# A decoder layer with 32 experts: order kept on chip, transfers of other rows set apart, last norms interleaved

## The chip, the core and the metric

The kernel runs on one core of a Trainium2 chip. The metric is the device time of one execution in microseconds, as the median of several. Engines: TensorE (PE), VectorE (DVE), ScalarE (ACT), GpSimd (POOL) and the queue of SyncE (SP). POOL issues the indirect DMAs (gathers and scatters by a list of row numbers), SP the plain ones.

## The reference

One layer: a projection, a pooling and a recurrent mixer, an output product with a layer norm (h), then a mixture of experts and a second layer norm. The change lies in the last two.

```python
def hierarchical_moe(h, ...):          # h: 4096 rows of 1024
    g_prob = softmax(h @ router_group + b_g)
    g_top_p, g_idx = lax.top_k(g_prob, 1)              # 1 of 4 groups
...
    e_top_logit, e_idx = lax.top_k(e_sel, 2)           # 2 of its 8 experts
    weights = g_top_p * softmax(e_top_logit)
...
    hid = silu(xb @ exp_gate[e]) * (xb @ exp_up[e])
    return (hid @ exp_down[e]) * wgt
...
h = layer_norm(ALPHA * x + mixed, ln1_g, ln1_b)
return layer_norm(ALPHA * h + hierarchical_moe(h), ln2_g, ln2_b)
```

## The kernel before

**Router.** `phase_out` goes over 32 blocks of 128 rows: two output products, the norm of h, then (one block later) transposes and the router's products. Each block writes h to `d_h` and ALPHA times h to `d_acc`. After a batch of blocks (`BATCHES`) `route` works out each row's group, two experts and weights on DVE, counts with two PE products, and POOL scatters small rows: (token, weight) into a table per expert (`d_tab`, two scatters a block) and the token into a list per group (`d_gtab`, one a block). The tiles `ids` and `row` that feed them have two buffers. Before the last batch `plan.order` ranks groups and experts by their counts so far; the ranks go out to `d_order` in memory and come back into `orow`, from which SP and POOL read which expert comes next.

**Experts.** `phase_moe` goes over the 32 ranks in a written order (`manual_schedule`): each engine runs the instructions in the order in which the code calls them. `GIVEN` and `GGIVEN` say how many blocks of 64 rows an expert of a rank, and of 128 rows a group, gets. For expert r: `fetch` gathers up to two blocks of finished rows of the group before from `d_acc` into `f_h`; `hidden` makes p_gu on PE, and in its gaps scales and stores (`out_dram`) the blocks fetched one expert earlier; `down` makes p_y, ACT evicts it to y, `scatter` adds y onto `d_acc`; beside it the rows of the next expert, gathered as `xg` (three buffers), are transposed on PE (m_pt) into xh (ACT) and xl (DVE), and DVE takes the statistics (`f_st`) of the fetched blocks. PE needs the last xl before the next p_gu.

The framework orders two accesses of `d_acc` by a wait unless told that they don't meet:

```python
def free(ins, others, reason):
    for other in others:
        if other is not last_pool[0]:
            tc.declare_no_dep(ins.ins, other.ins, reason=reason)
```

So each transfer still waits for the landing of the one issued just ahead of it.

**Last norms.** The last group has no expert after it: four blocks of it are fetched, and the six of `GGIVEN[-1]` are normalised one by one, with 1/sqrt as Ln and Exp on ACT (`log_root`, a table load before each), b2 added on POOL, a store, and one more fetch. Two loops that follow, for rows beyond the given counts, run zero times here; their branches make all engines meet.

## Time and profile before

| | |
|---|---|
| median of 3 runs | 3928.93 us (3922.88 to 3951.8) |
| profiled execution | 3922.84 us, span 3921.2 us, mean granted clock 0.883 |
| 0 to 2500: projection, mixer | PE busy 2178.37 us |
| 2500 to 2900: output product, router | PE busy 391.71 us, DMA share 0.64 |
| 2900 to 3000: end of router, first expert | PE busy 36.25 us, clock 0.61 |
| 3000 to 3850: experts | PE busy 739.96 us, clock 0.94, DMA share 0.79 |
| 3850 to 3921: last norms | PE busy 3.87 us, DVE 18.27, ACT 28.56, POOL 29.65 |

Stretches are in us from the span's start. The clock is the share of full speed that the throttle granted to PE, the DMA share the mean busy share of 16 DMA engines. In rows, the time in brackets is how long the engine was idle before the instruction, and behind the arrow what ended that; where it waited for several things the one named is the last by the profile.

### The profile page before, as it was taken

How to read it: one execution, taken by the hardware profiler on the slowest of the kernel's cores; microseconds unless marked ns; L12 is line 12 of the kernel's file. 1: busy time of each engine (PE TensorE's matmuls, PEld its weight loads, DVE VectorE, ACT ScalarE, POOL GpSimd, SP SyncE). 2: the span in 40 equal slices, each digit the busy share in tenths (PEclk: the TensorE clock that was granted, in tenths of full speed). 3: DMA queues.
4: the chain of work that ended last, by engine and by line, in shares of the span. 5: the costliest groups of instructions: out<-in, count | busy, mean ns of one | idle time of the engine just before them, and what ended most of it. 6: DMA issues, size and time to landing. Idle time of an engine off the chain costs nothing. (4 is left out here: it accounts for less than half of the span.)

```text
span 3921.2 us, 70586 instructions
## 1 busy us (share of the span) xinstructions
PE 3350.2 (85%) x27401; PEld 2801.9 (71%) x27401; DVE 1999.1 (51%) x4077; ACT 1620.8 (41%) x2718; POOL 1696.2 (43%) x2985
## 2 busy tenths in 40 slices
PE   7999999999857888888788886899976999697872
PEld 6887877777646776777677775677755898586762
DVE  2212231222256777667676673566553557546674
ACT  2212111111135455554545443565643555455444
POOL 3000030000157778777777783143432234534344
PEclk9999999999967788777878777999987999898886
DMA  7424252332223333343333323567636888777873
GB/s 253 177 116 182 99 186 102 119 127 94 68 57 72 84 73 83 68 87 70 80 76 75 86 57 94 185 142 156 145 76 180 214 232 260 225 218 231 233 235 101
DMA packets 509753, 531.22 MB, mean 135 GB/s; under 512 B 297853, under 2 KB 411687, under 8 KB 505320
## 3 DMA queue, kind: packets, MB, share of 16 engines
q1 hardware_dynamic: 445752, 367.94, 33.3%
q0 software_dynamic: 33920, 106.02, 10.8%
q10 hardware_dynamic: 29744, 52.73, 3.7%
q8 instruction: 216, 3.54, 0.4%
q14 instruction: 121, 0.99, 0.1%
HBM read 324.90 MB, written 206.92 MB: 136 GB/s over the span
## 5 line engine op out<-in xcount | busy, mean ns | idle before, releaser
L134 PE MATMUL acc<-xhi,wh 128*128 128x512 f32 x1408 | 565.8, 402 | 4.2 <-DVE zo L176 3.9
L135 PE MATMUL acc<-xlo,wh 128*128 128x512 f32 x1408 | 559.4, 397 | 0.0
L136 PE MATMUL acc<-xhi,wl 128*128 128x512 f32 x1408 | 559.4, 397 | 0.0
L491 POOL TENSOR_TENSOR db<-db,tmp 96x126 f32<-96x126 f32 (+22 forms) x992 | 456.4, 460 | 77.7
L176 DVE SCALAR_TENSOR_TENSOR zo<-acc,omu,zm 128x512 f32<-128x512 f32 x160 | 119.9, 750 | 661.1 <-ACT zm L173 617.7
L489 POOL TENSOR_TENSOR tmp<-db,gi 96x126 f32<-96x126 f32 (+22 forms) x992 | 423.1, 427 | 77.7
L173 ACT ACTIVATE zm<-acc,muc 128x512 f32<-128x512 f32 x160 | 110.2, 690 | 719.2 <-PE acc L136 717.9
L174 POOL COPY carry<-zm 128x1 f32<-128x1 f32 x160 | 30.8, 193 | 664.3 <-ACT zm L173 664.2
L134 PEld LDWEIGHTS acc<-xhi,wh 128*128 128x128 f32 x1408 | 265.4, 189 | 70.9 <-DVE zo L176 4.2
L135 PEld LDWEIGHTS acc<-xlo,wh 128*128 128x128 f32 x1408 | 265.7, 189 | 66.6 <-issue 3.8
L136 PEld LDWEIGHTS acc<-xhi,wl 128*128 128x128 f32 x1408 | 265.4, 188 | 63.4
L1262 POOL DMA_INDIRECT d_acc<-y,ix x81 | 136.9, 1690 | 282.6 <-DMA d_acc<-y,ix 73.2
L1061 PE MATMUL o_ps<-owh,mh 128*128 128x512 f32 x512 | 210.0, 411 | 18.1 <-ACT owh L889 17.6
L1314 PE MATMUL p_gu<-xl,wh_g 128*128 128x256 f32 (+4 forms) x512 | 159.2, 311 | 72.5 <-DVE xl L1293 72.5
L1061 PE MATMUL o_ps<-owh,ml 128*128 128x512 f32 x512 | 205.4, 401 | 5.0 <-POOL ml L876 5.0
L1061 PE MATMUL o_ps<-owl,mh 128*128 128x512 f32 x512 | 204.9, 401 | 0.4 <-DVE owl L890 0.3
L445 DVE TENSOR_TENSOR g<-tr,mask 128x384 f32<-128x384 f32 x256 | 130.2, 549 | 143.2 <-PE tr L443 143.2
L443 PE MATMUL tr<-ar,kb 64*128 64x128 f32 x1536 | 178.5, 364 | 25.5 <-DVE kb L430 17.4
L443 PEld LDWEIGHTS tr<-ar,kb 64*128 64x128 f32 x1536 | 147.3, 252 | 46.5 <-DVE g L445 17.3
L370 ACT ACTIVATE thw<-tr,chans 128x256 f32<-128x256 f32 x96 | 45.6, 475 | 297.6 <-PE tr L369 263.8
L1349 PE MATMUL p_y<-wh_d,hh 128*128 128x512 f32 (+1 forms) x324 | 145.5, 449 | 15.0 <-ACT hh L1324 15.0
L1314 PE MATMUL p_gu<-xh,wh_u 128*128 128x256 f32 (+4 forms) x512 | 157.9, 308 | 0.0
(354 smaller groups left out, 8704.1 us busy)
## 6 DMA issues: line engine op xcount, KB each, us to landing
d_rkv<-zo SPq DMA_DIRECT2D x144, 256.0 KB
ws<-in_exp_gate_dram SPq DMA_DIRECT2D x64, 512.0 KB
ws<-in_exp_up_dram SPq DMA_DIRECT2D x64, 512.0 KB
ws<-in_exp_down_dram SPq DMA_DIRECT2D x64, 512.0 KB
xq<-in_x_dram SPq DMA_DIRECT2D x32, 512.0 KB
d_xsp<-xhi ACTq DMA_DIRECT2D x8, 2048.0 KB
d_xsp<-xlo ACTq DMA_DIRECT2D x8, 2048.0 KB
xlo<-d_xsp SPq DMA_DIRECT2D x8, 2048.0 KB
```

The costliest lines, as they stand in the source:

```text
L134: nc.tensor.matmul(ps, lhsT=whi[i][:, k, :], rhs=xhi[:, k, :], start=k == 0, stop=False)
L135: nc.tensor.matmul(ps, lhsT=whi[i][:, k, :], rhs=xlo[:, k, :], start=False, stop=False)
L136: nc.tensor.matmul(ps, lhsT=wlo[i][:, k, :], rhs=xhi[:, k, :], start=False, stop=k == KD - 1)
L176: nc.vector.scalar_tensor_tensor(zo, ps, omu[:, ix:ix + 1], zm[:, :SEG], op0=OP.mult, op1=OP.add)
L443: nc.tensor.matmul(ps[h][:, p, :], lhsT=KB[hs, i, :], rhs=AR[hs, i, :], start=True, stop=True)
L445: nc.vector.tensor_tensor(G[:, h, c::NC, :], ps[h], masks[c % 2].unsqueeze(1).to_broadcast([128, 3, 128]), op=OP.mult)
L489: e.tensor_tensor(tm, Dh[:, :a, x:x + 1].to_broadcast([96, a, b]), G[:, x, x + 1:].unsqueeze(1).to_broadcast([96, a, b]), op=OP.mult)
L491: e.tensor_tensor(Dh[:, :a, x + 1:], Dh[:, :a, x + 1:], tm, op=OP.add)
L1061: nc.tensor.matmul(ps, lhsT=a[:, k, :], rhs=w[k][:, ns], start=k == 0 and i == 0, stop=k == KD - 1 and i == 2)
L1262: st = nc.gpsimd.indirect_dma_start(out=acc, out_offset=bass.IndirectOffsetOnAxis(ap=ix[:n, 0:1], axis=0), in_=y[:n], in_offset=None, boun ...
L1314: nc.tensor.matmul(p[:, :N], lhsT=a[:, k, fs], rhs=c[:, k, :N], start=k == 0 and i == 0, stop=k == KD - 1 and i == 2)
L1349: nc.tensor.matmul(ps[j][:a1 - a0], lhsT=x[:, a0:a1], rhs=w[:, f, n * 512:n * 512 + 512], start=f == 0 and i == 0, stop=f == NF - 1 and i ...
```

## The change

- `order` turns the two columns of ranks into two rows with PE products against the identity; DVE casts them into `orow` in SBUF. The trip through `d_order` goes. `BATCHES` ends 3, 3, 2 in place of 4, 3, 1, so that the order is made after 30 blocks in place of 31.
- `ids` and `row` get four buffers; the token column of `row` is one copy from a table (`token`) in place of an iota for each block and slot.
- The group-list scatters of the last two batches are put in `plan.later` and issued after the first three `xg` gathers, each behind a memset of one element.
- `free` drops the dependence on the transfer just ahead as well, and `apart` puts a memset of one element (`scr`) on POOL between two such transfers.
- The two copies of the last block's h (`keep`) stand after its transposes.
- The last group's six blocks are fetched at once, four into `f_h` and two into `y` buffers, and normalised in two threes with `root` (Newton steps on DVE, as in the other groups). b2 is added by DVE in every second block, and stores are interleaved with the second three.

```diff
-BATCHES = [4] * 7 + [3, 1]
+BATCHES = [4] * 6 + [3, 3, 2]
...
-    def order(self):
+    def order(self, ident, ps):
...
-        eoi = pool.tile([128, 2], I32, name="pl_eoi")
-        nc.vector.tensor_copy(eoi, eo)
-        nc.sync.dma_start(self.orderd, eoi)
+        for i in range(2):
+            nc.tensor.matmul(ps[:, i], lhsT=eo[:, i:i + 1], rhs=ident, start=True, stop=True)
+        nc.vector.tensor_copy(self.orow, ps)
...
-            ids = sm.tile([128, 3, QB, 1], I32, name="ids")
-            row = sm.tile([128, 2, QB, 2], I32, name="row")
+            ids = plan.pool.tile([128, 3, max(BATCHES), 1], I32, name="ids", bufs=4)
+            row = plan.pool.tile([128, 2, max(BATCHES), 2], I32, name="row", bufs=4)
+            nc.gpsimd.tensor_copy(row[:, :, :QB, 0], token[:, q0:q0 + QB].unsqueeze(1).to_broadcast([128, 2, QB]))
...
-                for q in range(QB):
-                    nc.gpsimd.iota(row[:, s, q, 0:1], pattern=[[0, 1]], base=(q0 + q) * 128, channel_multiplier=1)
...
+            for q in range(QB):
+                if q0 + QB < NQ - BATCHES[-1]:
+                    place(q)
+                else:
+                    plan.later.append(lambda q=q: place(q))
             if q0 + QB == NQ - BATCHES[-1]:
-                plan.order()
+                plan.order(ident, prt.tile([1, 2, 128], F32, name="prt"))
...
                 turn(q - LAG)
+                if q == NQ:
+                    keep(NQ - 1, h)
...
+        scr = cst.tile([1, 1], F32, name="scr")
+
+        def apart(*others):
+
+            if any(last_pool[0] is x for o in others for x in o):
+                nc.gpsimd.memset(scr, 0.0)
+
         def free(ins, others, reason):
             for other in others:
-                if other is not last_pool[0]:
-                    tc.declare_no_dep(ins.ins, other.ins, reason=reason)
+                tc.declare_no_dep(ins.ins, other.ins, reason=reason)
 
         def scatter(ix, y, n, g=None, same=()):
 
+            if g is not None:
+                apart(reads, same)
...
-            def fetch(self, n):
-                for _ in range(n):
-                    h = fp.tile([128, D], F32, name="f_h")
+            def fetch(self, n, tile=lambda i: fp.tile([128, D], F32, name="f_h")):
+                for i in range(n):
+                    h = tile(i)
+                    apart(*sums[self.g + 1:])
...
+            def put(self, h, b, add=True):
+                if add:
+                    nc.gpsimd.tensor_tensor(h, h, b2, op=OP.add)
+                else:
+                    apart(writes)
...
         for _ in range(3):
             ahead()
+        for place in plan.later:
+            nc.gpsimd.memset(scr, 0.0)
+            place()
+        last_pool[0] = None
...
-        norms.fetch(min(4, GGIVEN[-1]))
-        every = norms.new
-        while every or norms.b < GGIVEN[-1]:
-            norms.new = every[:1]
-            every = every[1:]
-            for x in norms.stats(log_root):
-                x()
...
+        tile = lambda i: fp.tile([128, D], F32, name="f_h") if i < 4 else hp.tile([128, D], F32, name="y", bufs=4)
+        while left:
+            some = min(left, 6)
+            left -= some
+            norms.fetch(some, tile)
...
+                nc.vector.tensor_tensor(h, h, g2, op=OP.mult)
+                if i % 2:
+                    nc.vector.tensor_tensor(h, h, b2, op=OP.add)
+                norms.put(h, b, i % 2 == 0)
...
+            for first in range(0, some, 3):
+                own = Norms(NG - 1, norms.ig)
+                own.new = every[first:first + 3]
+                pieces = own.stats(root)
+                n = len(own.got)
+                for i, x in enumerate(pieces):
+                    x()
+                    if i < n and ready:
+                        finish(ready.pop(0), done)
+                        done += 1
+                own.scale()
+                ready += own.got
```

**POOL among the experts.** Before, around one expert's two scatters, with the semaphores that each waits for (DMASW: an indirect DMA has landed, Activation: an eviction of y, DVE or Pool: that engine, PE: the transposes that free `xg`):

```order
L1262 DMA d_acc<-y,ix 4224x1024 [waits Activation_49]
L1262 DMA d_acc<-y,ix 4224x1024 [waits DMASW1_49,Activation_49]
L1389 DMA f_h<-d_acc,ig 128x1024 [waits DMASW2_49]
L1389 DMA f_h<-d_acc,ig 128x1024 [waits DMASW4_49]
L1432 TENSOR_TENSOR f_h<-f_h,b_28272 128x1024 [waits DVE_49]
L1433 DMA out_dram<-f_h,ig 4096x1024 [waits Pool_49]
L1248 DMA xg<-d_h,ix 128x1024 [waits DMASW6_49,PE_49]
L1248 DMA xg<-d_h,ix 128x1024 [waits DMAHW1_49,DMASW7_49,PE_49]
```

and after, at the same place in the expert's run (`L1282` is the scatter, `L1412` the gather, `L1455` the add, `L1458` the store):

```order
L1282 DMA d_acc<-y,ix 4224x1024 [waits DMASW3_49,DMASW1_49,Activation_49]
L1272 MEMSET scr 1x1
L1282 DMA d_acc<-y,ix 4224x1024 [waits DMASW2_49,Activation_49]
L1272 MEMSET scr 1x1 [waits Pool_49]
L1412 DMA f_h<-d_acc,ig 128x1024
L1412 DMA f_h<-d_acc,ig 128x1024 [waits DMASW5_49,DMASW4_49]
L1455 TENSOR_TENSOR f_h<-f_h,b_28211 128x1024 [waits DVE_49]
L1458 DMA out_dram<-f_h,ig 4096x1024 [waits Pool_49]
L1260 DMA xg<-d_h,ix 128x1024 [waits DMASW6_49,PE_49]
```

The order of transfers is the same, with a memset after each scatter. Before, the second scatter waits for the landing of the first and the first gather for that of the second; after, the second scatter waits for an older transfer and the first gather for none.

**POOL at the end of the router.** Before, from the iotas of the last but one batch on (`L1030` and `L1044` are the small scatters, `L1027` the iotas, `L1237` loads the first expert's list):

```order
L1027 IOTA row 128x1 x2
L1030 DMA d_tab<-row,ids 131072x2 x6
L1044 DMA d_gtab<-row,ids 16384x1 x3
L1030 DMA d_tab<-row,ids 131072x2 x2
L1044 DMA d_gtab<-row,ids 16384x1
L24 MEMSET m_id 128x128
L25 AFFINE_SELECT m_id<-m_id 128x128
L1196 TENSOR_LOAD orow
L1196 ISA x2
L1237 ISA
L1237 DMA ix<-d_tab 128x4x2
L1248 DMA xg<-d_h,ix 128x1024 x3
```

and after:

```order
L1032 DMA d_tab<-row,ids 131072x2 x6
L1047 DMA d_gtab<-row,ids 16384x1 x3
L1032 DMA d_tab<-row,ids 131072x2 x10
L24 MEMSET m_id 128x128
L25 AFFINE_SELECT m_id<-m_id 128x128
L1208 TENSOR_LOAD orow
L1208 ISA x2
L1249 ISA
L1249 DMA ix<-d_tab 128x4x2
L1260 DMA xg<-d_h,ix 128x1024 x3
L1500 MEMSET scr 1x1
L1047 DMA d_gtab<-row,ids 16384x1
```

The iotas that reuse the row buffer are gone from between the batches, and five group-list scatters (one of them shown) now stand between the third and the fourth `xg`, each behind a memset.

**DVE in the last norms.** Before, one block after the other:

```order
L1413 BN_STATS f_st<-f_h 128x6 x2
L1414 BN_AGGR f_mv<-f_st 128x2
L1417 SCALAR_TENSOR_TENSOR f_mr<-f_mv,f_ra 128x1
L1428 TENSOR_TENSOR f_h<-f_h,g_28271 128x1024
L1413 BN_STATS f_st<-f_h 128x6 x2
```

and after, the first three blocks (14 more small operations of the root follow, then the next block's statistics):

```order
L1436 BN_STATS f_st<-f_h 128x6 x2
L1437 BN_AGGR f_mv<-f_st 128x2
L1436 BN_STATS f_st<-f_h 128x6 x2
L1437 BN_AGGR f_mv<-f_st 128x2
L1436 BN_STATS f_st<-f_h 128x6 x2
L1437 BN_AGGR f_mv<-f_st 128x2
L1478 TENSOR_SCALAR f_va<-f_mv 128x3
L1479 TENSOR_SCALAR f_yi<-f_va 128x3
```

The statistics of three blocks now stand together ahead of one root, and no operation of ACT stands between a block's aggregation and its root.

## Rows read from the trace of the kernel before

**Rows 1.** waits in the expert phase, 2990 to 3850: engine line waited for, us, times, longest

```profile
DVE f_st L1413 <- DMA f_h<-d_acc,ig: 107.7, 25, 15.6
...
PE p_gu L1314 <- DVE xl L1293: 72.5, 13, 15.3
```

**Rows 2.** POOL's groups by line in 2990 to 3850: busy, mean ns, idle before

```profile
L1262 POOL DMA_INDIRECT d_acc<-y,ix x79 | 133.9, 1695 | 276.2 <-DMA d_acc<-y,ix 73.2 <-ACT y L1331 55.1 <-issue 45.4
...
L1389 POOL DMA_INDIRECT f_h<-d_acc,ig x28 | 29.3, 1045 | 87.8 <-DMA d_acc<-y,ix 84.7 <-issue 3.0
```

**Rows 3.** timeline of POOL, 3520 to 3550: start, us, instruction [idle before]

```profile
3524.81 1.59 POOL L1262 DMA_INDIRECT d_acc<-y,ix  x1 [0.30 <-issue]
3533.08 2.41 POOL L1262 DMA_INDIRECT d_acc<-y,ix  x1 [6.68 <-ACT wh_g L1226]
3543.40 1.43 POOL L1262 DMA_INDIRECT d_acc<-y,ix  x1 [7.90 <-ACT y L1331]
3548.30 1.00 POOL L1389 DMA_INDIRECT f_h<-d_acc,ig  x1 [3.47 <-DMA d_acc<-y,ix]
```

**Rows 4.** timeline of ACT, 3520 to 3530

```profile
3525.97 0.68 ACT L1331 ACTIVATE y<-p_y,ix 64x512 f32<-64x512 f32 x1 [0.65 <-PE p_y L1349]
```

**Rows 5.** timeline of DVE, 3550 to 3592

```profile
3552.56 1.29 DVE L1413 BATCH_NORM_STATS2 f_st<-f_h 128x6 f32<-128x512 f32 x2 [8.92 <-DMA f_h<-d_acc,ig]
...
3587.49 0.16 DVE L1449 TENSOR_SCALAR f_va<-f_mv 128x2 f32<-128x2 f32 x1
...
3590.50 0.16 DVE L1417 SCALAR_TENSOR_TENSOR f_mr<-f_mv,f_ra 128x2 f32<-128x2 f32 x1
```

**Rows 6.** timeline of PE, 3552 to 3590

```profile
3555.30 0.58 PE L1314 MATMUL p_gu<-xl,wh_g 128*128 128x256 f32 x1 [7.12 <-DVE xl L1293]
...
3587.63 0.58 PE L1314 MATMUL p_gu<-xl,wh_g 128*128 128x256 f32 x1 [12.15 <-DVE xl L1293]
```

**Rows 7.** busy time by stretch, with granted clock, DMA share and rate

```profile
3560.00:3575.00 15.00, 15.00 (x110) 13.78 (x109) 9.16 (x12) 9.29 (x16) 4.17 (x2) 1.00 0.97 314
...
3587.00:3594.00 7.00, 6.37 (x34) 6.37 (x35) 6.48 (x21) 3.26 (x4) 1.92 (x2) 0.58 0.98 243
```

**Rows 8.** DMA in 2990 to 3850, by queue

```profile
DMA packets 67955, 192.83 MB, mean 224 GB/s; under 512 B 21046, under 2 KB 21046, under 8 KB 67889
...
q0 software_dynamic: 27776, 95.81, 45.3%
q1 hardware_dynamic: 39825, 95.13, 32.8%
```

**Rows 9.** timeline of POOL, 2905 to 2985

```profile
2910.55 1.00 POOL L1030 DMA_INDIRECT d_tab<-row,ids  x1 [22.63 <-DVE rks L1040]
...
2937.67 0.20 POOL L1027 IOTA row<- 128x1 int32 x2 [11.69 <-DMA d_gtab<-row,ids]
...
2964.15 0.83 POOL L1237 DMA_DIRECT2D ix<-d_tab  x1 [8.57 <-DMA d_tab<-row,ids]
...
2977.85 0.91 POOL L1248 DMA_INDIRECT xg<-d_h,ix  x1 [7.30 <-PE m_pt L1276]
```

**Rows 10.** timeline of PE, 2930 to 2990

```profile
2975.64 4.01 PE L1276 MATMUL m_pt<-m_id,xg 128*128 128x128 f32 x20 [36.29 <-DMA ws<-in_exp_up_dram]
...
2983.96 0.74 PE L1314 MATMUL p_gu<-xh,wh_g 128*128 128x448 f32 x1
```

**Rows 11.** timeline of POOL, 3848 to 3922

```profile
3858.81 1.43 POOL L1262 DMA_INDIRECT d_acc<-y,ix  x1 [5.37 <-issue]
...
3894.88 2.33 POOL L1432 TENSOR_TENSOR f_h<-f_h,b 128x1024 f32<-128x1024 f32 x1 [3.52 <-SPq L1570]
...
3909.24 0.98 POOL L1433 DMA_INDIRECT out_dram<-f_h,ig  x1 [0.28 <-POOL f_h L1432]
```

**Rows 12.** timeline of DVE, 3848 to 3922

```profile
3867.03 1.29 DVE L1413 BATCH_NORM_STATS2 f_st<-f_h 128x6 f32<-128x512 f32 x2 [17.65 <-DMA f_h<-d_acc,ig]
...
3871.96 1.23 DVE L1428 TENSOR_TENSOR f_h<-f_h,g 128x1024 f32<-128x1024 f32 x1 [1.36 <-ACT f_h L1424]
```

More of the change, by code (lines that the diff above doesn't have):

```diff
@@ L722, with __init__ @@
 class Plan:
-    def __init__(self, tc, pool, orderd, restd):
+    def __init__(self, tc, pool, restd):
         nc = self.nc = tc.nc
-        self.pool, self.orderd, self.restd = pool, orderd, restd
+        self.pool, self.restd = pool, restd
+        self.orow = pool.tile([1, 2, 128], I32, name="orow")
+        self.later = []
         self.ones = pool.tile([128, 128], F32, name="pl_ones")
@@ L1041, in route, with place @@
             nc.vector.scalar_tensor_tensor(r, gi, float(CAP), r, op0=OP.mult, op1=OP.add)
-            nc.vector.tensor_copy(ids[:, 2, :, 0], r)
-            for q in range(QB):
+            nc.vector.tensor_copy(ids[:, 2, :QB, 0], r)
+            def place(q):
                 st = nc.gpsimd.indirect_dma_start(
@@ L1066, in norm, with keep @@
             h = state[q][3]
+            ln_rows(nc, sm, h, leps, g1, b1)
+        def keep(q, h):
             t0 = q * 128
-            ln_rows(nc, sm, h, leps, g1, b1)
             hk = hp.tile([128, KD, 128], F32, name="hk")
@@ L1119, in phase_out @@
             if 0 <= q - LAG < NQ:
+                h = state[q - LAG][3]
                 turn(q - LAG)
+                if q == NQ:
+                    keep(NQ - 1, h)
             if q < NQ:
@@ L1123, in phase_out @@
                 norm(q)
+                if q < NQ - 1:
+                    keep(q, state[q][3])
             b = q - LAG - 1
@@ L1404, in stats @@
                     return []
-                st = sm.tile([128, 2, 2, 6], F32, name="f_st")
-                mv = sm.tile([128, 2, 2], F32, name="f_mv")
-                ra = sm.tile([128, 2], F32, name="f_ra")
-                mr = sm.tile([128, 2], F32, name="f_mr")
+                st = sm.tile([128, 4, 2, 6], F32, name="f_st")
+                mv = sm.tile([128, 4, 2], F32, name="f_mv")
+                ra = sm.tile([128, 4], F32, name="f_ra")
+                mr = sm.tile([128, 4], F32, name="f_mr")
                 self.ra, self.mr = ra, mr
@@ L1428, in apply @@
                     nc.vector.tensor_tensor(h, h, g2, op=OP.mult)
+            def put(self, h, b, add=True):
[3 more added lines that the diff above has]
+                    apart(writes)
+                st = nc.gpsimd.indirect_dma_start(
+                    out=o, out_offset=bass.IndirectOffsetOnAxis(ap=self.ig[:, b:b + 1], axis=0),
+                    in_=h, in_offset=None, bounds_check=S - 1, oob_is_err=False)
+                free(st, writes, "other rows of the result")
+                last_pool[0] = st
+                writes.append(st)
             def store(self):
                 for h, b in self.got:
-                    nc.gpsimd.tensor_tensor(h, h, b2, op=OP.add)
-                    st = nc.gpsimd.indirect_dma_start(
-                        out=o, out_offset=bass.IndirectOffsetOnAxis(ap=self.ig[:, b:b + 1], axis=0),
-                        in_=h, in_offset=None, bounds_check=S - 1, oob_is_err=False)
-                    free(st, writes, "other rows of the result")
-                    last_pool[0] = st
-                    writes.append(st)
+                    self.put(h, b)
                 self.got = []
         def root(mv, ra, n):
-            va = sm.tile([128, 2], F32, name="f_va")[:, :n]
-            yi = sm.tile([128, 2], I32, name="f_yi")[:, :n]
-            tm = sm.tile([128, 2], F32, name="f_tm")[:, :n]
+            va = sm.tile([128, 4], F32, name="f_va")[:, :n]
+            yi = sm.tile([128, 4], I32, name="f_yi")[:, :n]
+            tm = sm.tile([128, 4], F32, name="f_tm")[:, :n]
             rs = ra[:, :n]
@@ L1510, in phase_moe, with finish @@
         norms = Norms(NG - 1)
-        norms.fetch(min(4, GGIVEN[-1]))
-        every = norms.new
-        while every or norms.b < GGIVEN[-1]:
-            norms.new = every[:1]
-            every = every[1:]
-            for x in norms.stats(log_root):
-                x()
-            norms.scale()
-            norms.apply()
-            norms.store()
-            if norms.b < GGIVEN[-1]:
-                norms.fetch(1)
-                every += norms.new
+        left = GGIVEN[-1]
+        tile = lambda i: fp.tile([128, D], F32, name="f_h") if i < 4 else hp.tile([128, D], F32, name="y", bufs=4)
[3 more added lines that the diff above has]
+            norms.fetch(some, tile)
+            every, ready = norms.new, []
+            norms.new = []
+            def finish(x, i):
+                h, b = x
+                nc.vector.tensor_tensor(h, h, g2, op=OP.mult)
+                if i % 2:
+                    nc.vector.tensor_tensor(h, h, b2, op=OP.add)
+                norms.put(h, b, i % 2 == 0)
+            done = 0
+            for first in range(0, some, 3):
[10 more added lines that the diff above has]
+                ready += own.got
+            for x in ready:
+                finish(x, done)
+                done += 1
         manual.close()
@@ L1573, in phase_moe @@
             again.new = [(h, None)]
-            for x in again.stats(log_root):
+            for x in again.stats(root):
                 x()
@@ L1594, in body @@
         gtab = dp.tile([NG * CAP, 1], I32, name="d_gtab")
-        orderd = dp.tile([128, 2], I32, name="d_order")
         restd = dp.tile([128, 4], I32, name="d_rest")
```

29 lines of the change are left out of this document (11 added, 18 removed).

## The prediction

> **What bounds the kernel now.** I read the table of waits over the expert phase first, because a share of busy time over the whole program mixes stages with different limits. TensorE (PE) waits 72.5 us there, 13 times, for one thing: the low halves of the next expert's rows (xl), which VectorE (DVE) writes before the first product p_gu [rows 1]. DVE is late because it runs in order and, ahead of the last xl, stands at the statistics of a fetched block (f_st), for which it waits 107.7 us in 25 pieces [rows 1].
>
> Why the fetched block is late is read from GpSimd (POOL), grouped by line: it sat idle for 276.2 us ahead of its 79 scatter-adds (d_acc, L1262) and for 87.8 us ahead of its 28 gathers (f_h, L1389) [rows 2]. The names of the releasers are to be read with care. In one stretch the three scatter-adds of an expert are issued at 3524.81, 3533.08 and 3543.40, the gather at 3548.30 [rows 3]. The last eviction of that expert's y began at 3525.97 and took 0.68 [rows 4], so ScalarE, weights and evictions named there had long been done; what is left for each scatter is the landing of the one ahead of it. The statistics start at 3552.56, after 8.92 of waiting [rows 5], and PE at 3555.30, after 7.12 [rows 6]. POOL runs one expert late, and PE pays.
>
> Two more stretches stand by themselves. Between router and experts PE is idle for 36.29 us up to the first transposes at 2975.64, and its first product is at 2983.96 [rows 10]. At the end the first statistics start at 3867.03 [rows 12] and the last store is issued at 3909.24 [rows 11]: 43 us in which nothing but six blocks is normalised, one after the other.
>
> **Part 1, the expert phase.** The change puts a memset of one element between a scatter-add and the transfer behind it, and drops the dependences on the transfer just ahead. By the order of waits, the second and third scatter of an expert and the first gather then wait for nothing newer than the expert before. In the stretch above the three scatters would go out at 3524.81, about 3526.8 and 3528.8, and the gather at about 3530.5, 18 us earlier. Even if it landed as late as 12 us after issue (an estimate from 3552.56 minus 3548.30 = 4.3 seen there, times almost three) it would be there at 3542.5, ten before DVE asks. So the 72.5 us should go nearly whole: two thirds of the DVE stall of 107.7 is what PE sees, and no other engine stands in the same place.
>
> The stall is paid a second time in the clock. After PE's wait of 12.15 that ends at 3587.63 [rows 6] the granted clock averages 0.58 over 7 us, against 1.00 in 3560 to 3575 [rows 7]: between the levels of 1.2 and 2.4 GHz, nearer the lower, so 7 x 0.42 = 2.9 us lost. Four or five of the 13 waits are long enough for that, and shorter ones lose some; I put 13 us on it. Together 72.5 + 13 = 85.
>
> The memsets are 56 on POOL. No row has a memset of one element; POOL's small operations at the boundary take 0.20 [rows 9], and POOL has 364 us of idle time in this phase, so 56 x 0.2 = 11 us is hidden. If POOL's slack were gone it would cost those 11.
>
> Against the 85 stands DMA. The transfers of the 860 us moved 192.83 MB, with 45.3% of the 16 engines' time in POOL's queue, 32.8% in SP's and 0.9% in others: 79%, or 679 us of work that does not shrink [rows 8]. In 775 us that is a share of 0.88, in 795 it is 0.85. PE ran without a gap through 3560 to 3575 at a share of 0.97 [rows 7], so 0.88 is possible but for arrivals that bunch: weights and gathers will be later than now. I take 20 off: 65. The bounds are 25 (only as much as a share of 0.81 allows) and 95 (85 and some of the waits for ScalarE, which a filled clock also shortens).
>
> One rule of the Trainium skill gives another sum. The rows say that 314 GB/s went with a share of 0.97 [rows 7], so that some 324 would be all there is for this mixture of packets. The Trainium skill's page "DMA: Bandwidth & Descriptors", section "Specifications", puts the limits at about 358 GB/s for one core's HBM traffic and 435 for the fabric. By the page 192.83 MB need no more than 539 us, DMA would never be near its limit at 249 GB/s, nothing comes off the 85, and the sum of all parts would be 3922.84 - 110 = 3813. The measured share decides against it: by the rows it is 3922.84 - 90.
>
> **Part 2, from the router to the experts.** Of the twelve small scatters of one batch the first is issued at 2910.55, each issue taking about 1 us, and POOL is released only at 2937.67, when the last of them has landed, because the next batch reuses their row buffer [rows 9]: 27.1 / 12 = 2.26 us of service each, more than their issue. DVE is held by the same buffer. Then 12 more scatters go out and the list of the first expert is loaded at 2964.15: 26.5 us, 2.2 each [rows 9]. The change gives four buffers (the wait of 11.69 goes) and takes 5 of the group-list scatters (d_gtab), four of which stand among those 12, out of the way: 4 x 2.26 = 9.0. The sum is 20.7. DVE must still do the ranking, now for two last blocks with the order ahead of them, and the expert order now costs two PE products and a DVE copy on chip in place of a round trip that was hidden; I give 3 back, so the first transposes move 17.7 earlier, to about 2958. Now the cover is gone: the five deferred scatters stand behind the third gather, ahead of the fourth. They need 5 x 2.26 = 11.3 us of the queue, where POOL before waited 7.30 for PE [rows 9]; with the part of their time that lies beyond the first gathers I charge 5.7. The first product then moves 12 earlier. The ends: 5 (the ranking comes no earlier and only the group lists leave) and 18 (the queue lets the fourth gather by).
>
> The later copies of the last block (keep behind turn), POOL's copy in place of iotas and the smaller last batches lie beside PE's products or POOL's waits; I take nothing for them, and 2 us either way within these ends if they do not.
>
> **Part 3, the last norms.** Before, from the first statistics to the end of the last store: 3909.24 + 0.98 - 3867.03 = 43.2 us [rows 11, 12]. After, DVE carries it: six blocks of statistics at 1.29 [rows 12] and 0.2 for their aggregation (an estimate from the small operations of [rows 5, 9]) = 8.9; two roots of 15 small operations, from 3587.49 to 3590.50 and 0.16 more, 3.2 each [rows 5], = 6.4; six multiplications of 1.23 [rows 12] = 7.4; three adds of the same shape = 3.7. That is 26.4. The stop at the loop's branch, 3.52 on POOL [rows 11], stays; 1.2 is waiting for ScalarE's scaling (taken from the like-sized multiplication) and 1.0 the last store: 32.1, a gain of 11. ScalarE's table loads go, but they lay in that same chain and are not counted again. The scatter ahead no longer waits 5.37 for its neighbour [rows 11]; its own eviction allows some 3 of that. With 1 back for two more gathers ahead: 13, between 6 (POOL's adds and stores still set the pace) and 16.
>
> **The sum.** 3922.84 - 65 - 12 - 13 = 3832.8 for an execution such as the profiled one. The median of the three runs is 3928.93, 6.1 above it, so the forecast is 3839.
>
> **Rivals.** (a) DMA binds: the freed engines ask for the same 679 us of transfers in less time and meet late weights. Speaks for it: 0.79 already as a mean, two queues that both matter [rows 8]. Against: the stretch at 0.97 without a gap [rows 7]. If 0.82 is all that can be held on average, the phase takes 679 / 0.82 = 828, a gain of 32, and the whole is 3922.84 - 57 + 6 = 3872. (b) The waits move rather than go: the first scatter of each expert still waits for the scatters of the expert before, and gathers still queue behind them, so POOL stays late and DVE's stall remains to nine tenths. For it: those dependences are in the new order; against: a full expert, 20 us or more, lies between. Gain 7 + 25: 3897. (c) DMA takes nothing back: a share of 0.88 is below 0.97 [rows 7], no transfer comes late, and the whole 85 is kept: 3922.84 - 110 + 6 = 3819. The limits of the Trainium skill's page, above, come to the same. (d) Slower: scatters that overlap slow each other. POOL's queue has 390 us of engine time now, the rest 290 [rows 8]. If its packets came to take k times as long, DMA alone would last the present 860 us from k = 1.46 on; at 1.7 it lasts 953, and with 25 gained elsewhere the kernel ends at 3922.84 + 68 + 6 = 3997. For it: the scatter-adds ran singly so far, so no row excludes it. Against: the wait behind them was 8 to 10 us each [rows 3] at an issue of 2, as of transfers that share the engines with weights and not of ones that fill them.
>
> **How the numbers follow.** Forecast 0.55, (a) 0.19, (b) 0.10, (c) 0.12, (d) 0.04. The range of 3795 to 3893: the low end is all three upper bounds, 95 + 18 + 16 = 129 off, less some 5 for the runs' spread; the high end all lower bounds, 25 + 5 + 6 = 36 off. It leaves out (d) and most of (b). One per cent of 3928.93, 39 us, is about what a measurement of this kernel can tell from no change, so faster begins below 3890: the forecast, (c) and nearly all of (a), 0.84; the same: (b) and the rest of (a), 0.12; slower: (d), 0.04.
>
> **What would show it.** In the profile after: DVE's wait at f_st below 20 us and PE's at p_gu for xl below 15; POOL's idle ahead of d_acc down by over half and then named after evictions; the DMA share of the phase at 0.84 to 0.88; the first product near 2972; the last store some 30 us behind the first statistics. New rows of PE waiting for weights or xg of over 20 us would mean (a), f_h still landing after DVE asks (b), a higher time for the same packets in POOL's queue (d). The prediction is wrong above all if PE's 72.5 us reappear under another name.

## The result, and the profile after

| | before | after |
|---|---|---|
| median | 3938.53 us (4 runs, 3922.88 to 3951.8) | 3837.02 us (4 runs, 3826.27 to 3845.02) |
| profiled execution | 3922.84 us, span 3921.2, clock 0.883 | 3845.02 us, span 3843.4, clock 0.888 |

The ratio is 0.9742, 95% interval 0.9689 to 0.9795: faster. The fourth run of before, 3948.14 us, was made beside the runs of after.

The two spans in stages, cut at instructions of TensorE (PE). The last two columns are a later pair of profiles from one and the same chip (runs c0 and c1, below).

| stage, us | before | after | before, c0 | after, c1 | forecast |
|---|---|---|---|---|---|
| output product, first to last o_ps | 463.4 | 480.5 | 461.9 | 460.7 | same |
| last o_ps to first p_gu | 81.3 | 72.6 | 77.7 | 67.0 | -12 |
| first p_gu to last p_y (experts) | 869.6 | 791.9 | 873.6 | 789.3 | -65 |
| last p_y to the end | 67.6 | 58.5 | 67.8 | 58.8 | -13 |

**The experts.** The table of waits of the kernel after, 2985 to 3800 (engine, line, what it waits for; us, times, longest), answers to [rows 1]:

```profile
PE p_y L1369 <- ACT hh L1344: 18.5, 15, 4.9
PE p_y L1369 <- DVE hl L1345: 16.6, 8, 2.4
...
DVE f_st L1436 <- DMA f_h<-d_acc,ig: 15.1, 3, 13.7
...
PE m_pt L1296 <- DMA xg<-d_h,ix: 9.3, 2, 7.2
...
PEld p_gu L1334 <- DVE xl L1313: 0.2, 1, 0.2
```

The 72.5 us at p_gu for xl are gone. The 15.1 at f_st lie in the last norms (the window reaches into them); among the experts VectorE (DVE) never waits for a fetched block. What PE still waits for is mainly hh and hl, the high and low halves of the hidden rows, which ACT and DVE write ahead of p_y; 7.2 of the 9.3 for a gather of xg lie ahead of the first product. GpSimd's (POOL's) groups by line, 2985 to 3800, against [rows 2]: the scatter-adds' idle time fell from 276.2 to 91.7 us and is named after evictions, the gathers' from 87.8 to 11.1. The idle time now stands ahead of xg, where POOL waits for PE's transposes: POOL is early.

```profile
L1282 POOL DMA_INDIRECT d_acc<-y,ix x81 | 126.7, 1564 | 91.7 <-ACT y L1351 79.7 <-ACT xh L1312 8.7 <-issue 3.3
L1260 POOL DMA_INDIRECT xg<-d_h,ix x76 | 82.6, 1087 | 292.9 <-PE m_pt L1296 287.1 <-issue 3.0 <-PE p_y L1369 2.7
...
L1412 POOL DMA_INDIRECT f_h<-d_acc,ig x32 | 47.1, 1473 | 11.1 <-issue 8.8 <-DMA d_acc<-y,ix 2.3
L1272 POOL MEMSET scr<- 1x1 f32 x53 | 31.2, 588 | 0.0
```

One expert on POOL's timeline, 3515 to 3550, against [rows 3]: the scatters stand 3.65 us apart instead of 8.27 and 10.32, and the gather 1.9 behind the last.

```profile
3530.59 1.62 POOL L1282 DMA_INDIRECT d_acc<-y,ix  x1 [1.05 <-ACT y L1351]
3531.63 0.61 POOL L1272 MEMSET scr<- 1x1 f32 x1
3534.24 1.59 POOL L1282 DMA_INDIRECT d_acc<-y,ix  x1 [2.00 <-ACT y L1351]
3535.26 0.61 POOL L1272 MEMSET scr<- 1x1 f32 x1
3536.13 2.04 POOL L1412 DMA_INDIRECT f_h<-d_acc,ig  x1 [0.26 <-issue]
```

DMA in 2990 to 3785, against [rows 8]: POOL's queue and SP's together 84.0% of the engines' time, the share that was forecast (0.84 to 0.88).

```profile
DMA packets 68630, 194.90 MB, mean 245 GB/s; under 512 B 21217, under 2 KB 21217, under 8 KB 68563
...
q0 software_dynamic: 28353, 97.48, 48.1%
q1 hardware_dynamic: 39922, 95.53, 35.9%
```

**The boundary.** POOL after, 2905 to 2990, and PE, 2930 to 3000, against [rows 9, 10]:

```profile
2941.13 0.96 POOL L1032 DMA_INDIRECT d_tab<-row,ids  x1 [16.20 <-DVE rks L1042]
...
2959.79 0.96 POOL L1032 DMA_INDIRECT d_tab<-row,ids  x1 [11.01 <-DVE rks L1042]
...
2968.35 0.84 POOL L1249 DMA_DIRECT2D ix<-d_tab  x1 [2.15 <-issue]
...
2974.80 1.00 POOL L1047 DMA_INDIRECT d_gtab<-row,ids  x1 [0.23 <-issue]
...
2981.41 0.93 POOL L1260 DMA_INDIRECT xg<-d_h,ix  x1 [0.51 <-issue]
```

```profile
2979.19 5.45 PE L1296 MATMUL m_pt<-m_id,xg 128*128 128x128 f32 x24 [21.61 <-POOL scr L1500]
2991.86 1.08 PE L1296 MATMUL m_pt<-m_id,xg 64*128 64x64 f32 x8 [7.22 <-DMA xg<-d_h,ix]
2992.99 0.74 PE L1334 MATMUL p_gu<-xh,wh_g 128*128 128x448 f32 x1
```

POOL no longer waits for its own scatters but for DVE's ranking (rks), and it stands idle for 2.15 us ahead of the list's load instead of 8.57. From first transposes to first product, though, 13.8 us pass instead of 8.3: the gather behind the five group lists comes last.

**The last norms.** POOL and DVE after, 3780 to 3840, against [rows 11, 12]:

```profile
3815.33 2.33 POOL L1455 TENSOR_TENSOR f_h<-f_h,b 128x1024 f32<-128x1024 f32 x1 [1.33 <-DVE f_va L1478]
...
3826.30 2.47 POOL L1455 TENSOR_TENSOR y<-y,b 128x1024 f32<-128x1024 f32 x1
3829.05 1.67 POOL L1458 DMA_INDIRECT out_dram<-y,ig  x1 [0.28 <-POOL y L1455]
...
3831.02 0.99 POOL L1458 DMA_INDIRECT out_dram<-y,ig  x1 [0.21 <-POOLq L1618]
```

```profile
3794.51 1.28 DVE L1436 BATCH_NORM_STATS2 f_st<-f_h 128x6 f32<-128x512 f32 x2 [13.74 <-DMA f_h<-d_acc,ig]
...
3800.72 0.17 DVE L1479 TENSOR_SCALAR f_yi<-f_va 128x3 int32<-128x3 int32 x1
...
3809.30 2.15 DVE L1551 TENSOR_TENSOR f_h<-f_h,g 128x1024 f32<-128x1024 f32 x1
...
3815.35 2.33 DVE L1479 TENSOR_SCALAR f_yi<-f_va 128x3 int32<-128x3 int32 x1
...
3826.61 3.24 DVE L1553 TENSOR_TENSOR y<-y,b 128x1024 f32<-128x1024 f32 x1
```

From the first statistics to the end of the last store it is 3831.02 + 0.99 - 3794.51 = 37.5 us, before 43.2, forecast 32.1. The two f_yi rows show one reason: the same operation on three numbers a partition takes 0.17 alone and 2.33 when it starts beside an addition of POOL, as long as that addition.

### The profile page after: what moved, and what is told of

The parts are those of the page before. It is cut to its first block, busy times and chain, and to the rows that moved or that the text cites. A ratio compares the mean times of both kernels' runs of the same rounds, so it can differ in the third digit from the quotient of the medians.

```text
span 3843.4 us, 70576 instructions
## 1 busy us (share of the span) xinstructions
PE 3346.6 (87%) x27405; PEld 2800.3 (73%) x27405; DVE 2041.7 (53%) x4105; ACT 1600.2 (42%) x2694; POOL 1728.8 (45%) x2988
## 3 DMA queue, kind: packets, MB, share of 16 engines
q0 software_dynamic: 33920, 106.02, 10.7%
## 5 line engine op out<-in xcount | busy, mean ns | idle before, releaser
L489 POOL TENSOR_TENSOR tmp<-db,gi 96x126 f32<-96x126 f32 (+22 forms) x992 | 430.0, 433 | 77.7
L1260 POOL DMA_INDIRECT xg<-d_h,ix x81 | 87.4, 1079 | 296.7 <-PE m_pt L1296 288.0
L443 PE MATMUL tr<-ar,kb 64*128 64x128 f32 x1536 | 180.3, 367 | 24.2 <-DVE kb L430 16.6
L1282 POOL DMA_INDIRECT d_acc<-y,ix x81 | 126.7, 1564 | 91.7 <-ACT y L1351 79.7
L879 POOL TENSOR_TENSOR ml<-m,mh 128x1024 fp32r<-128x1024 f32 x32 | 76.6, 2395 | 184.4 <-ACT mh L878 184.3
```

The source lines that it names most:

```text
L443: nc.tensor.matmul(ps[h][:, p, :], lhsT=KB[hs, i, :], rhs=AR[hs, i, :], start=True, stop=True)
L489: e.tensor_tensor(tm, Dh[:, :a, x:x + 1].to_broadcast([96, a, b]), G[:, x, x + 1:].unsqueeze(1).to_broadcast([96, a, b]), op=OP.mult)
L1282: st = nc.gpsimd.indirect_dma_start(out=acc, out_offset=bass.IndirectOffsetOnAxis(ap=ix[:n, 0:1], axis=0), in_=y[:n], in_offset=None, boun ...
```

## The experiments

Times of one group share a chip and the runs of the kernel before on it. "Experts", "boundary" and "tail" are the stages of the table.

**a1 to a4: the parts alone** (kernel before there: 3926.43). a1 is the kernel before with part 1 only:

```diff
+        scr = cst.tile([1, 1], F32, name="scr")
...
+        def apart(*others):
...
+            if any(last_pool[0] is x for o in others for x in o):
+                nc.gpsimd.memset(scr, 0.0)
...
         def free(ins, others, reason):
             for other in others:
-                if other is not last_pool[0]:
-                    tc.declare_no_dep(ins.ins, other.ins, reason=reason)
+                tc.declare_no_dep(ins.ins, other.ins, reason=reason)
...
         def scatter(ix, y, n, g=None, same=()):
...
+            if g is not None:
+                apart(reads, same)
...
                     h = fp.tile([128, D], F32, name="f_h")
+                    apart(*sums[self.g + 1:])
```

> The kernel before with the memsets and the dropped dependences alone. If the waits of POOL for landings are what holds DVE and then PE, the expert phase (first p_gu to last p_y, 870 us before, 802 after) falls to about 802 here too, DVE's wait at f_st to under 5 us, and the kernel gains 65 to 70 us (ratio about 0.983). Rival: the gain of the phase comes from the other parts or from the state of the executions; then the phase stays above 850 and the ratio above 0.99.

a2 is the kernel after without part 1, but for the stores: those of finished blocks (`out_dram`) don't wait for one another.

```diff
-        def free(ins, others, reason):
+        def free(ins, others, reason, last=False):
             for other in others:
-                tc.declare_no_dep(ins.ins, other.ins, reason=reason)
+                if last or other is not last_pool[0]:
+                    tc.declare_no_dep(ins.ins, other.ins, reason=reason)
...
-            if g is not None:
-                apart(reads, same)
...
-                    apart(*sums[self.g + 1:])
...
-                free(st, writes, "other rows of the result")
+                free(st, writes, "other rows of the result", True)
```

> The changed kernel with the dependence on the transfer just ahead kept and no memsets among the experts. If the three parts are separate, the expert phase is back at 865 to 875 us, DVE waits about 108 us at f_st and PE about 72 us for xl, and the kernel is 22 to 30 us faster than before (ratio 0.992 to 0.995). Rival: the parts overlap, and the ratio falls below 0.985 or rises to 1.

a3 is a2 with the last norms as before (`log_root`, one block after the other), a4 is a2 with the router and the boundary as before (`BATCHES`, `d_order`, iotas, no `later`).

> The kernel before with the router part alone (order on chip, batches 3, 3, 2, four row buffers, deferred group lists, copies of the last block behind its transposes). From the end of the last output product to the first p_gu: 81.1 us before, 64.2 after. If the profile's difference is the part's worth, 64 to 66 here, a gain of 12 to 18 us (ratio about 0.996). Rival: the later end of the output products in the profile after (2920 in place of 2903) belongs to this part, so that it gains nothing: ratio 0.999 to 1.003 and products that end near 2920 again.

> The kernel before with the last norms alone (six blocks fetched at once, roots on DVE, stores interleaved). From the last p_y to the end of the span: 67.2 us before, 57.5 after. Expected 57 to 59 here, a gain of 8 to 13 us (ratio 0.997). Rival: without the dropped waits the second scatter is late as before and the gain is 5 or less.

| | median us | ratio, 95% | experts | boundary | tail |
|---|---|---|---|---|---|
| a1 part 1 | 3836.24 | 0.9768, 0.9751 to 0.9784 | 786.1 | 78.0 | 64.7 |
| a2 parts 2 and 3 | 3891.11 | 0.9912, 0.9895 to 0.9928 | 860.7 | 67.6 | 61.3 |
| a3 part 2 | 3899.53 | 0.993, 0.9913 to 0.9947 | 860.7 | 67.5 | 66.9 |
| a4 part 3 | 3909.45 | 0.9955, 0.9939 to 0.9972 | 864.0 | 78.6 | 60.1 |

In the expectations of a1 and a3 the figures "after" of 802 and 64.2 us are misread: cut as in the table above, the kernel after has 791.9 and 72.6. All four kernels gained more than was expected of them: 90, 35, 27 and 17 us, where 65 to 70, 22 to 30, 12 to 18 and 8 to 13 stood.

Part 1 alone takes the experts to where the whole change has them, so they are its doing: in a1 DVE doesn't wait at f_st among the experts and PE not for xl, while in a2 to a4 PE waits 64 to 71 us for xl. No run drops the waits without the memsets, so what these do for the order isn't shown. Part 2 shortens the boundary by 10.7 us (the mean of a1 and a4 less that of a2 and a3), part 3 the tail by 5.6 (a3 to a2). Part 1 has some 2 of the tail as well (a3 to a1). The products of the ratios, 0.9768 x 0.9912 = 0.968, are less than the change's own, 0.974: the experts of a2 to a4, with part 1 out, are 6 to 13 us shorter than the 870 to 874 of before, and the product counts that twice. That is a part of the some 22 us between the two; the rest stays open. The stores' wait that they drop is the only piece of part 1 that all three share; that it makes those us was not tried apart.

**b0 to b3** (kernel before there: 3945.84). b0 is the kernel after once more.

> The changed kernel once more, beside the next three and with a second profile. In the first profile the stage of output products took 480 us, in the kernel with the waits kept, whose router part is the same, 458. If that is the state of one execution, 456 to 466 here and a span of 3820 to 3830; if it belongs to the change as a whole, 475 to 485 again and 3840 to 3850.

b1 gives all additions of b2 to DVE:

```diff
-                    nc.gpsimd.tensor_tensor(h, h, b2, op=OP.add)
-                else:
-                    apart(writes)
+                    nc.vector.tensor_tensor(h, h, b2, op=OP.add)
+                apart(writes)
```

> The changed kernel with every add of b2 on VectorE in place of GpSimd, in the expert phase and in the last norms. In the profile after, hl of 128x256 took 1191 ns in place of 425 and wl_g 1540 in place of 1221, beside GpSimd's adds of 2.7 us. Theory (VectorE and GpSimd hold each other up while both work on SBUF): hl returns to 430 and wl_g to 1230, PE's waits for hl and hh fall by some 10 us, and the last norms end 3 to 5 us earlier: 8 to 15 us faster than the changed kernel. Rival (VectorE is merely fuller): 28 adds of 1.22 more on it, the waits grow by 10 and the kernel is 0 to 15 us slower.

b2 loads only the first half of each down-projection weight and uses it twice, which leaves out the second half:

```diff
+                    if n == "d" and i:
+                        RAW[r, n, 1] = RAW[r, n, 0]
+                        continue
```

> The changed kernel with the second half of each expert's down weights not loaded (the first half is used twice, so the output is another one): 16 MB fewer, 8% of the bytes of the expert phase. If DMA holds the phase up (the 20 us that the prediction took off), the phase shortens by 15 to 25 us. Rival (DMA is hidden): the phase changes by less than 4 us while the DMA share falls from 0.85 to about 0.79.

b3 puts the five deferred group lists behind all gathers of the first expert:

```diff
-        for place in plan.later:
-            nc.gpsimd.memset(scr, 0.0)
-            place()
-        last_pool[0] = None
...
         for _ in rows(0):
             pass
+        for place in plan.later:
+            nc.gpsimd.memset(scr, 0.0)
+            place()
+        last_pool[0] = None
```

> The changed kernel with the five deferred group-list scatters behind the gathers of the first expert in place of behind the third of them. The prediction charged 5.7 us for their place ahead of the fourth gather. If so, from the end of the output products to the first p_gu 4 to 7 us less than in the changed kernel (67.6 there without the waits' part). Rival: the fourth gather waits for PE anyway: less than 1.5 us.

| | median us | ratio, 95% | experts | boundary | tail |
|---|---|---|---|---|---|
| b0 the change | 3855.71 | 0.9778, 0.9741 to 0.9815 | 787.1 | 73.5 | 58.1 |
| b1 additions on DVE | 3831.32 | 0.9699, 0.9663 to 0.9735 | 771.3 | 73.0 | 55.5 |
| b2 half the down weights | 3845.29 | 0.9753, 0.9714 to 0.9793 | 786.0 | 74.1 | 57.5 |
| b3 lists later | 3840.52 | 0.9739, 0.9705 to 0.9773 | 784.3 | 66.3 | 59.0 |

b2 decides on DMA. The experts of b0, then of b2 (busy us of PE, its weight loads, DVE, ACT and POOL with counts; clock, DMA share, GB/s):

```profile
2997.10:3784.20 787.10, 747.49 (x4660) 657.38 (x4660) 554.54 (x975) 443.63 (x661) 374.01 (x292) 0.97 0.85 247
```

```profile
3000.80:3786.80 786.00, 749.28 (x4660) 658.40 (x4660) 554.29 (x975) 443.29 (x661) 373.55 (x292) 0.97 0.82 226
```

247 to 226 GB/s, 16.6 MB less, and 1.1 us: the rival of the expectation, that DMA is hidden, holds. In b0 PE waits only 0.7 us for a gather among the experts. The share fell to 0.82 and not to the 0.79 that was expected, so it did not follow the bytes.

b1 shows what does. DVE's groups by form in 2990 to 3790, of the kernel after and of b1 (busy us, mean ns | idle before; wl_g is the low half of a weight):

```profile
L1239 DVE TENSOR_TENSOR wl_g<-ws,wh_g 128x1024 fp32r<-128x1024 f32 x62 | 95.5, 1540 | 6.2 <-ACT wh_g L1238 6.2
...
L1345 DVE TENSOR_TENSOR hl<-sg,hh 128x256 fp32r<-128x256 f32 x20 | 23.8, 1191 | 9.7 <-ACT hh L1344 8.2 <-issue 1.5
L1345 DVE TENSOR_TENSOR hl<-sg,hh 128x192 fp32r<-128x192 f32 x14 | 21.0, 1502 | 6.0 <-ACT hh L1344 5.6 <-issue 0.4
```

```profile
L1239 DVE TENSOR_TENSOR wl_g<-ws,wh_g 128x1024 fp32r<-128x1024 f32 x62 | 75.8, 1222 | 15.1 <-ACT wh_g L1238 15.1
...
L1345 DVE TENSOR_TENSOR hl<-sg,hh 128x256 fp32r<-128x256 f32 x20 | 8.5, 425 | 9.7 <-ACT hh L1344 8.7 <-issue 1.0
L1345 DVE TENSOR_TENSOR hl<-sg,hh 128x192 fp32r<-128x192 f32 x14 | 5.0, 358 | 6.0 <-ACT hh L1344 5.2 <-issue 0.9
```

The same subtraction takes 425 ns in b1, where POOL adds nothing, and 1191 on average in the kernel after. In the kernel before, POOL made the same 28 additions and it took 425 too (same window):

```profile
L1325 DVE TENSOR_TENSOR hl<-sg,hh 128x256 fp32r<-128x256 f32 x20 | 8.5, 425 | 9.7 <-ACT hh L1324 9.7
```

Counted over the timelines of the experts, 16 of DVE's statistics (f_st), 20 xl and 7 hl ran beside an addition of POOL there; in the kernel after it was no statistics and no xl, but 19 hl and 13 wl_g. The change itself moved POOL's additions onto hl and wl_g. In the three groups above DVE spent 51.0 us more in the kernel after than in b1; b1's 28 additions cost it 33.3. PE's wait for hl, 16.6 us in b0, is gone in b1, while its wait for hh grew from 17.6 to 23.3; why that grew was not followed. The stages of b1 are 18.9 us shorter than b0's (experts 15.8, tail 2.6, boundary 0.5), the medians 24.4, where 8 to 15 was expected: the theory that the two engines hold each other up holds, the rival of a merely fuller DVE falls. b0's output product was long again, 485.1, as its expectation had it for the theory that this belongs to the change; the next group answers that. b3 is read below, with the prediction.

**c0 to c3, a third chip** (kernel before there: 3920.9). c0 is the kernel before and c1 the kernel after, both unchanged:

> The kernel before, profiled again on the chip of the next three, for the output projection (first to last product o_ps). It took 463.4 us in the kernel before, 458 to 464 in the four kernels with one part each, and 480 to 497 in the five profiles of the changed kernel and its variants, none of which was on the same chip as a profile of before. Theory that the longer projection is the chip's or the moment's: it is as long here as in the next run, within 5 us, whatever that is. Theory that the change itself lengthens it: 458 to 466 here and 478 or more in the next. The rest as in the kernel before: 80 us from there to the first product p_gu, 868 for the experts, 67 from the last product to the end.

> The changed kernel once more, as the reference of the next two: ratio 0.974 to 0.978. Output projection 480 or more if it is the change's, and equal to the run above within 5 us if it is the chip's; if it is 460 here and in the run above, the ratio should fall to about 0.970, as the product of the single parts' ratios has it (0.9768 x 0.9912 = 0.968). Boundary 68 to 74, experts 786 to 792, tail 58.

c2 has the edits of b1 and b3 together:

> The changed kernel with both edits that helped alone: the last norm's additions and those of all experts on VectorE, and the deferred group lists behind the first expert's gathers. Theory that the two are independent: boundary 7 us shorter (66), experts 771, tail 55.5, together some 25 to 28 us under the changed kernel, ratio about 0.967. Rival, that the lists, pushed into the first expert, hold up its second-next gathers, and that this shows once VectorE no longer does: experts 778 or more, and no more than 20 us together.

c3 puts eight memsets where the change puts one:

```diff
-                nc.gpsimd.memset(scr, 0.0)
+                for _ in range(8):
+                    nc.gpsimd.memset(scr, 0.0)
```

> The changed kernel with eight memsets of one element in each gap instead of one: some 390 more on GpSimd, at 0.6 us each (as in the changed kernel's phase) 235 us of work in a phase of 790. Theory that GpSimd has slack and what hurts is only its additions beside VectorE's two-input operations: experts no longer than 795, with the time for hl no higher than in the run with one memset. Theory that the memsets too hold VectorE up, or that GpSimd's slack is used: experts at 800 to 850, the wait at f_st back, hl slower than 1.2 us.

| | median us | ratio, 95% | output product | experts | boundary | tail |
|---|---|---|---|---|---|---|
| c0 before | 3926.59 (one run) | | 461.9 | 873.6 | 77.7 | 67.8 |
| c1 the change | 3819.65 | 0.9737, 0.972 to 0.9755 | 460.7 | 789.3 | 67.0 | 58.8 |
| c2 additions and lists | 3784.54 | 0.9656, 0.9637 to 0.9675 | 461.5 | 768.4 | 60.6 | 56.1 |
| c3 eight memsets | 3816.24 (one run) | | 459.2 | 790.7 | 66.9 | 59.8 |

The output product is as long with the change as without it, on one chip. So the 17.1 us by which it was longer in the profile after are not put down to the change; the kernel before, run beside that profile, took 3948.14 as well. What lengthened it there, and in b0 to b3 (485 to 497), stays open; PE's clock in it was 0.95 in the profile after and 0.97 in c0 and c1. c1's ratio stayed at 0.974 and did not fall to the 0.970 that was expected for this case.

c2 is the fastest, 35.1 us under c1 by the medians, 30.0 by the stages: the two edits add up (20.9 experts, 6.4 boundary, 2.7 tail; the forecast of 25 to 28 was low, the rival of 778 for the experts fell). c3's experts are 1.4 us longer than c1's in one profile each, far from 800. The expected 0.6 us a memset was wrong too; POOL's timeline of c3:

```profile
3310.70 1.62 POOL L1283 DMA_INDIRECT d_acc<-y,ix  x1 [0.48 <-ACT y L1352]
3311.74 1.64 POOL L1273 MEMSET scr<- 1x1 f32 x8
```

Eight take 1.64 us where one took 0.61 (timeline of after, above), so 0.15 for each further one. The record of the first begins inside that of the scatter ahead of it, so its 0.6 us seem to be mostly the scatter's end. All memsets among c3's experts come to 63.6 us of POOL's time, those of c1 to 31.4: the run added 32 us of work, not 235, and so tests POOL's slack far less than was meant. Its hl of 128x256 took 905 ns, c1's 1140: the memsets do not hold DVE up.

## Why the prediction was right, and where it was off

**Part 1: the mechanism held, the DMA term failed.** The forecast was 72.5 of waiting and 13 of clock, 85, less 20 for DMA. On one chip the experts, c0 and then c1:

```profile
2983.60:3857.20 873.60, 762.94 (x4660) 677.27 (x4660) 519.56 (x975) 445.71 (x661) 336.90 (x239) 0.93 0.79 223
```

```profile
2969.40:3758.70 789.30, 750.37 (x4660) 659.48 (x4660) 553.72 (x975) 443.44 (x661) 373.82 (x292) 0.96 0.85 246
```

PE's wait for xl, in c0's table of waits for 2984 to 3855,

```profile
PE p_gu L1314 <- DVE xl L1293: 77.9, 13, 15.9
```

has no row in c1's, and the same 4660 products take 762.94 - 750.37 = 12.6 us less at a clock of 0.96 instead of 0.93. That is the clock term as forecast. Together 90.5 us were released. PE's wait for hl took 11.3 back (5.6 in c0, 16.9 in c1), its wait for a gather of xg gave 8.5 more (10.7 to 2.2), and its other waits took 2.6: 85.1, beside the 84.3 measured. The 20 taken off for DMA were the wrong step: b2 shows 1.1 us for 8.5% of the bytes. The argument for them was that some 324 GB/s is all that this mixture of packets can have and that arrivals would bunch. The kernel after moved 334 GB/s in a stretch where PE had hardly a gap, and c2 held a share of 0.88 over its whole expert phase, the share that was feared for 775 us, in 768.4:

```profile
3540.00:3560.00 20.00, 19.84 (x145) 17.85 (x144) 18.48 (x36) 14.01 (x20) 11.29 (x11) 1.00 0.99 334
```

```profile
2960.70:3729.10 768.40, 739.46 (x4660) 653.11 (x4660) 530.72 (x1003) 443.22 (x661) 285.74 (x284) 0.98 0.88 253
```

So (c) was the better account of this phase, and (a) and (b) fell: no new wait for weights, none at f_st. (d) fell as well: the two queues take 84.0% of 795 us, 668, where they took 78.1% of 860, 672 [rows 8], so overlapping scatters did not take more of the engines' time; each landed a little later (median 7.7 us from its issue in c1, 7.0 in c0). The Trainium skill's page "DMA: Bandwidth & Descriptors", section "Specifications", by whose limits of some 358 and 435 GB/s nothing would come off, gave the better sum for the experts; the measured share that was set against it was no evidence that DMA would bind.

What was taken back, the wait for hl, is due to POOL's additions: without them it is gone in b1, whose experts are 15.8 us shorter than b0's. The prediction had no term for it.

One reading of it was off without harm: a block landing at 3542.5 would not be there ten us before DVE asks, but one, since DVE stood from 3552.56 - 8.92 = 3543.64 on [rows 5].

**The memsets** were costed at nothing beside POOL's idle time, and c3 agrees as far as it goes: some 390 more of them, 32 us of work, change nothing that one profile can show.

**Part 2 held in its two sums, not in each term.** c0 to c1, from the last o_ps to the first transposes: 70.7 to 53.6 us, 17.1 less (forecast 17.7); from there to the first product 7.0 to 13.4, 6.4 more (charged 5.7): 10.7, forecast 12. But the 17.7 was 11.7 for the buffers and 9.0 for the lists, less 3 for the ranking, and the 9.0 did not come: from the first scatter of the last but one batch to the load of the list it is 2968.35 - 2941.13 = 27.2 us in the profile after, where it was 26.5 [rows 9], although 10 scatters stand there in place of 12: POOL now waits 11.01 for DVE's ranking in between. The gain is the earlier start of that batch, 18.3 us from c0 to c1 (33.8 to 15.5 behind the end of the last o_ps). That the total fitted is luck, and which of the router's edits moved the start was not tried apart. That the charge is the group lists' is shown by b3, where PE has them out of its way:

```profile
2983.76 5.45 PE L1296 MATMUL m_pt<-m_id,xg 128*128 128x128 f32 x24 [21.85 <-issue]
2989.97 0.68 PE L1296 MATMUL m_pt<-m_id,xg 64*128 64x64 f32 x8 [0.76 <-DMA xg<-d_h,ix]
```

7.1 us to the first product at 2990.9, as before the change, and a boundary 7.2 shorter than b0's. The "first product near 2972" came at 2993.0 in the profile after, since the output product ended 17.7 later there; in c1 it came at 2969.4.

**Part 3: right in kind, too large.** 13 was forecast, 9.1 came (9.0 in c1). The gathers' side gave 3.8 (last p_y to first statistics 13.4 to 9.6; forecast 3). The mis-sized term is the sum of 32.1 for the norms, 37.5 measured. Of the missing 5.4, 3.1 are two DVE operations beside POOL's additions: f_yi 2.33 for 0.17 and one multiplication 2.15 for 1.17. The last addition took 3.24 for 1.22 as well, but the last store did not wait for it: it ended at 3829.85, and POOL's own addition (2.47) and store (1.67) ahead of the last store went on to 3830.72. So at the end POOL sets the pace, which the sum, made of DVE's operations, left out. The durations of that sum came from rows in which DVE worked alone. c2's DVE, with no addition on POOL, has them back:

```profile
3760.31 0.17 DVE L1478 TENSOR_SCALAR f_yi<-f_va 128x3 int32<-128x3 int32 x1
...
3770.78 1.23 DVE L1552 TENSOR_TENSOR y<-y,b 128x1024 f32<-128x1024 f32 x1
```

Three more additions on DVE there, and 34.6 us in all.

**The sum** fitted better than its terms, and that is luck. In the profile after, the experts gave 12.7 us more than forecast, boundary and tail 7.2 less, and the output product, on which the change has no part, took 17.1 more: the profiled execution came 12.2 above the sum. The median of the kernel after then lies 8.0 below its profiled execution, where the forecast had put it 6.1 above; the two cancel, and 3839 stands 2 us from 3837.02. On the third chip the medians differ by 101.3 us, where the sum was 90.

## What to carry to other kernels

Where an in-order engine issues transfers that need not wait for one another, look for the wait that is paid one expert later by another engine, and add the clock that the idle time costs: together they were the gain, to within a few us. In this kernel a mean DMA share of 0.85, and of 0.88 in c2, was no reason to take anything off: no row showed PE waiting for weights. Halving one load showed it in a single run. A faster engine also shifts the work behind it: ask what its operations will stand beside. Before giving VectorE and GpSimd work at the same time, take the durations from rows where both are busy, not from rows where one is alone.

## What the runs showed of the hardware that was not expected

DVE and POOL hold each other up, but not on every operation. A DVE operation on 128x3 numbers took 2.33 us instead of 0.17 beside an addition of POOL, a 128x256 subtraction 1191 ns on average instead of 425, and POOL's additions 2716 ns instead of 2460 in the kernel before (28 of each). b1 and c2, without those additions, are 24.4 and, with the lists moved, 35.1 us faster.

Which operations are held shows in two rows beside an addition each. In the kernel before xl, which subtracts from PE's product m_pt, takes its usual 0.68 (mean 0.685):

```profile
3552.95 2.38 POOL L1432 TENSOR_TENSOR f_h<-f_h,b 128x1024 f32<-128x1024 f32 x1
```

```profile
3554.57 0.68 DVE L1293 TENSOR_TENSOR xl<-m_pt,xh 128x512 fp32r<-128x512 f32 x1
```

In the kernel after hl of 128x192, which reads two tiles that DVE and ACT wrote (sg, hh), ends 0.2 behind POOL's addition; in b1 it took 0.36:

```profile
3778.16 2.40 POOL L1455 TENSOR_TENSOR f_h<-f_h,b 128x1024 f32<-128x1024 f32 x1
```

```profile
3778.45 2.33 DVE L1345 TENSOR_TENSOR hl<-sg,hh 128x192 fp32r<-128x192 f32 x1 [0.43 <-ACT hh L1344]
```

Over the experts of the kernel before, the statistics beside an addition took 688 ns and the others 681, xl of 128x512 took 681 and 685. In the kernel after the 7 hl of 128x256 beside one took 2.6 us on average, the other 13 took 426 ns. Which engine is held differs: DVE's multiplication of f_h by g, which also reads two tiles, ran ten times beside an addition there and took its usual 1.22, while nine of these additions took 3.3 and not 2.4. What decides it no run shows.

The Trainium skill's page "GPSIMD Engine Reference", section "Specifications", says that GpSimd's interfaces to SBUF are shared with VectorE, with contention where a VectorE instruction reads two SBUF inputs or runs in a two-port mode. The rows of hl and xl agree with the first case; in which mode f_yi, with its one input, ran, no row shows. The size, up to the whole of POOL's operation, is the rows'.
